# Index keys' tile moved to another buffer, and the loads around the GLU products reordered

## The chip, the cores and the metric

The kernel runs on one core of a Trainium2 chip. Time is device time in microseconds (us). Engines: TensorE (PE, matmuls and transposes), VectorE (DVE), ScalarE (ACT), GpSimd (POOL) and SyncE (SP, which issues nearly all DMAs here, in order). Matmul operands lie in SBUF, products come out in PSUM.

## The reference

One step of a one-layer hybrid encoder over 1024 prompt tokens and 32 sample tokens, width 1024. What matters here:

```python
h = rms_norm(x, g_norm) * (1 + scale) + shift
u, zs, q, k, v, za, qi, ki, wi, gm = split(h @ w_in)
ys = gelu(ssm(u))                              # 512 channels
ys = ys * sigmoid(ys @ w_glu + b_glu)          # GLU products
ys = ys * silu(zs)                             # silu factor
logits = relu(qi . [cache_kidx, ki]) / 8       # indexer, 8 heads of 64
score  = sum_heads(wi * logits)                # then the best 256 (136) keys per query
ya = attention(q, chosen k, v) * silu(za)
out = (sigmoid(g_s) * (ys @ w_ps) + sigmoid(g_a) * (ya @ w_pa)) @ w_o
```

## The kernel before

All products with float32 accuracy are made of three matmuls: each operand is a high part (rounded to the PE's fp32r format) plus a low part, and `mm3` adds high x high, high x low, low x high. Splitting costs a cast for the high part (`wh`, `ygH`, `yo[0]`, mostly on ScalarE) and a subtraction for the low part (`wl`, `ygL`, `yo[1]`, on VectorE or GpSimd).

A stream of jobs `Z` (class Stream) feeds PE. A Job is one product of 128 columns of a weight with all 1056 tokens, in 3 chunks of 352 columns; a chunk is 24 matmuls (8 row blocks x 3), for the GLU products 12 (4 x 3). Two PSUM buffers `pz` alternate, so a chunk can start when an evacuation one or two chunks earlier is done. While a job runs, the weight of the next one is split and that of the one after is loaded.

The stretch that the change touches comes after the SSM. There the jobs run in this order: `ki` (index keys and head weights, 72 columns, evacuated by ScalarE into the tile `zki`, L1073), `qi0` (index queries, evacuated by two copies on ScalarE and two subtractions on VectorE, L1066 to L1069), `glu0` to `glu3`, `qi1`. For the GLU, the four tiles y (128 channels each, gelu of the SSM's output) have been stored to DRAM (L991, `yD`) and are loaded again in token order (L1115, `yg`), then split into `ygH` and `ygL` (L70, L73). `gate_tile(q)` loads the two parts of silu(zs), stored by the silu jobs earlier (`zsD` is zs, `ztD` its tanh, made in tiles `zt` and `zth`), makes the silu factor z2 = (t2 + 1) * zs (L1089) and multiplies it by y (L1091). After each GLU chunk ScalarE takes the tanh (L1101), VectorE multiplies it in (L1102), and the product is split into `yo` (ScalarE and GpSimd) and stored (L1106). z2 has two buffers: tiles 2 and 3 are loaded at the end of glu0 and glu1 (`gate_tile(q + 2)`).

During qi1 PE transposes the cached index keys, loaded into `cki` (L1169, 128 partitions with pieces of 256 bytes, twice), and `zki` (L1174, L1183). `kid` collects all index keys, `kiH` and `kiL` are its parts, and the indexer's products follow (L1206, L1207). Pieces of w_mod are loaded between (`rpiece`, L1147) for a gate row (`grow`, L1155). Then a threshold search counts scores on ScalarE and VectorE (L1541, L1543); GpSimd clears its small tiles (L1518 to L1528).

PE's order is the order of the code (manual schedule). From L1038 to the search, the orders of SP, ACT, DVE and POOL are set by a scheduler from the code and a timeline that it works out, so a change of code moves instructions on all of them. Pools are stacks of SBUF: `kp` is opened when the SSM's pools have been closed, on the same bytes, so its first users wait for the last readers of what lay there. `stg` stays open for the whole kernel.

Of the kernel before, what the change touches and what calls it, by code (L numbers as in the profile page):

```python
# [7 lines left out]
F32 = mybir.dt.float32  # L8
# [9 lines left out]
NT = T + TS  # L18
# [40 lines left out]
def body(nc, tc, I, O, dbg=None):  # L59
    ctx = ExitStack()  # L60
    dbg = dbg or (lambda name, ap: None)
    I = {k: v for k, v in I.items()}
    te, ve, se, ge, sp = nc.tensor, nc.vector, nc.scalar, nc.gpsimd, nc.sync

    def f32(ap):
        return ap.bitcast(F32)

    def split(h, l, src, heng, leng):
        if heng is se:
            se.copy(h, src)  # L70
        else:
            heng.tensor_copy(h, src)
        leng.tensor_sub(l, src, f32(h))  # L73
# [3 lines left out]
    stg = ctx.enter_context(tc.tile_pool(name="stg", bufs=2))  # L77
# [613 lines left out]
    def silu_job(name, c0, dst, heng, leng, th_dst=None):  # L691

        def begin():
            zt = stg.tile([128, NT], F32, tag="stg", name="zt")
            zth = stg.tile([128, NT], F32, name="zth", bufs=1) if th_dst is not None else None

            def ev(n, ps):
                if th_dst is not None:
                    se.activation(zth[:, ns(n)], ps, AF.Tanh, scale=0.5)
                    se.copy(zt[:, ns(n)], ps)  # L700
                else:
                    th = stg.tile([128, G3], F32, tag="sth", name="th")
                    se.activation(th, ps, AF.Tanh, scale=0.5)
                    ve.scalar_tensor_tensor(zt[:, ns(n)], th, 1.0, ps, op0=ALU.add, op1=ALU.mult)
                if n == 2:
                    sp.dma_start(dst, zt)
                    if th_dst is not None:
                        sp.dma_start(th_dst, zth)
            return ev
        return Job(name, wcol(c0), begin, heng=heng, leng=leng)  # L710
# [343 lines left out]
    ysD = [[dram.tile([128, NT], F32, name=f"ys{h}D{q}") for q in range(4)] for h in "HL"]  # L1054
    stK = ExitStack()
    kp = stK.enter_context(tc.tile_pool(name="kp", bufs=1, side="right", reuse_waits="tile"))
    zki = kp.tile([72, NT], F32)
    QS = {}

    def qijob(j):  # L1060
# [18 lines left out]
    def tok(t):  # L1079
        return ((t[:, 0:1024].rearrange("p (c s) -> p c s", s=8), slice(0, 128)),  # L1080
                (t[:, 1024:NT].rearrange("p (c s) -> p c s", s=8), slice(129, 133)))

    yg, Z2 = [], []

    def gate_tile(q):
        z2, t2 = (gp.tile([128, NT], F32, name=n, bufs=b) for n, b in (("z2", 2), ("t2", 1)))
        sp.dma_start(z2, zsD[q])
        sp.dma_start(t2, ztD[q])
        ve.scalar_tensor_tensor(z2, t2, 1.0, z2, op0=ALU.add, op1=ALU.mult)  # L1089
        for v_, c in tok(z2):  # L1090
            ve.tensor_mul(v_, v_, yg[q][:, c])  # L1091
        Z2.append(z2)

    def glu_job(q):
        def begin():
            z2 = Z2[q]

            def ev(n, ps):
                c = ns(n)
                th = stg.tile([128, G3], F32, tag="sth", name="th")  # L1100
                se.activation(th, ps, AF.Tanh, scale=0.25, bias=bglu[:, q:q + 1])  # L1101
                ve.scalar_tensor_tensor(z2[:, c], th, 1.0, z2[:, c], op0=ALU.add, op1=ALU.mult)  # L1102
                yo = [gp.tile([128, G3], F32R, name=f"yo{h}", bufs=3) for h in range(2)]
                split(yo[0], yo[1], z2[:, c], se, ge)
                for h in range(2):
                    sp.dma_start(ysD[h][q][:, c], f32(yo[h]))  # L1106
                if n == 2 and q < 2:
                    gate_tile(q + 2)
            return ev
        return Job(f"glu{q}", w_glu[:, 128 * q:128 * q + 128], begin, kt=4, heng=se, leng=ve,  # L1110
                   rhs=lambda n, k: (ygH[k][:, ns(n)], ygL[k][:, ns(n)]))

    for q in range(4):
        yg.append(gp.tile([128, 8, NCH], F32, name=f"yg{q}").rearrange("p s c -> p c s"))
        sp.dma_start(yg[q].rearrange("p c s -> p s c"), yD[q])  # L1115
        for (h_, c), (l_, _) in zip(tok(ygH[q]), tok(ygL[q])):
            split(h_, l_, yg[q][:, c], se, (ge, ve)[(YS >> q) & 1])
    w_glu = I["w_glu"].rearrange("o d e -> (o d) e")
    for q in range(2):
        gate_tile(q)  # L1120
    Z.add(*(glu_job(q) for q in range(4)), qijob(1), *(gate_job(f, se, ve) for f in range(NS, NI - 1)))
    Z.add(qijob(2), qijob(3), gate_job(NI - 1, se, ve), hold=True)
    Z.until("glu3")
# [10 lines left out]
    ip = stI.enter_context(tc.tile_pool(name="ip", bufs=1, side="right", reuse_waits="tile"))  # L1134
# [28 lines left out]
    for hf_ in range(2):  # L1163
        sp.dma_start(kid[64 * hf_:64 * hf_ + 64, 0:1024], zki[0:64, 0:1024])
        sp.dma_start(kid[64 * hf_:64 * hf_ + 64, 1536:1568], zki[0:64, 1024:1056])
    cki = ip.tile([128, 4, 2, 64], F32)
    ckd = I["cache_kidx"].rearrange("a b (k p) d -> p (a b k) d", p=128)
    for hf_ in range(2):
        sp.dma_start(cki[:, :, hf_], ckd)  # L1169
    rpiece(0, None)  # L1170
    run(KF)
    pt = ps_t()
# [22 lines left out]
    for j in range(4):  # L1195
# [3 lines left out]
        for i in range(2, 9):  # L1199
            t0, m, k0, nk = (128 * i, 128, 0, 128 * (i + 1)) if i < 8 else (1024, 32, 1024, 544)  # L1200
            for e in range(2):
                h = 2 * j + e
                ps = ps_s()
                for a in range(0, nk, 512):
                    b = min(nk, a + 512)
# [468 lines left out]
    for k in range(len(seq) + 3):  # L1674
        it = at(k)
        if k in first:
            p, begin = first[k]
# [229 lines left out]
```

## Time and profile before

| what | value |
|---|---|
| time, median of 3 runs (lowest to highest) | 1058.91 us (1058.77 to 1058.99) |
| the profiled execution: its own time, its span | 1059.41 us, 1057.6 us |
| PE busy, share of the span | 996.2 us, 94% |
| DVE, ACT, POOL busy | 769.6, 541.9, 247.2 us |
| mean granted clock of PE, share of full speed | 0.98 |

How to read it: busy time of PE is from the start of a matmul to its modelled end, so back-to-back matmuls overlap and the step from one start to the next is the time that one takes. The granted clock is 1.00 at 2.4 GHz and 0.50 at 1.2 GHz. In a timeline, the bracket behind an instruction is how long its engine was idle before it and what ended that, as inferred.

### The profile page before, as it was taken

Reading aid. Unit: us, or ns where it says so; the run is one execution under the profiler, and the core shown is the slowest. Engines: PE = TensorE matmul, PEld = TensorE weight load, DVE = VectorE, ACT = ScalarE, POOL = GpSimd, SP = SyncE. Lnnn points to the kernel's source line nnn. Section 1 sums busy time; section 2 is a strip of 40 time slices with the busy share of each in tenths; the row PEclk is TensorE's granted clock in tenths of the full one; section 3 lists DMA queues with packets and bytes.
Section 4 is the critical chain, followed back from the end, with each engine's and each line's share of the span. In section 5 each row is a group of like instructions: output and inputs, shape, how many; then the busy total and the mean of one; then the engine's idle time right before and its main releaser. Section 6 shows DMA issues by size and latency. Waiting matters only on the chain.

```text
span 1057.6 us, 17197 instructions
## 1 busy us (share of the span) xinstructions
PE 996.2 (94%) x6194; PEld 927.6 (88%) x6194; DVE 769.6 (73%) x1756; ACT 541.9 (51%) x1164; POOL 247.2 (23%) x467
## 2 busy tenths in 40 slices
PE   4999999998979999898898999999999999999997
PEld 3899999997878889898898998899898988998786
DVE  4669798985755979988889945756657776786534
ACT  3642344545335656868895336655556555434111
POOL 3202400000240013243313442333222231340000
PEclk8999999998989999999998999999999999999999
DMA  9922722236673212223232242242133622854311
GB/s 304 273 69 85 228 77 79 78 102 196 196 231 111 61 61 73 79 71 111 81 101 83 81 144 56 77 131 61 51 101 106 222 80 76 277 162 139 123 67 60
DMA packets 125329, 126.00 MB, mean 119 GB/s; under 512 B 14400, under 2 KB 104980, under 8 KB 125244
## 3 DMA queue, kind: packets, MB, share of 16 engines
q1 hardware_dynamic: 124864, 124.59, 38.2%
q8 instruction: 49, 0.80, 0.3%
q14 instruction: 36, 0.29, 0.1%
q10 hardware_dynamic: 220, 0.28, 0.1%
q0 software_dynamic: 160, 0.03, 0.0%
HBM read 87.81 MB, written 36.50 MB: 118 GB/s over the span
## 4 chain that ended last, share of the span: by engine, by line
PE 65%; DVE 10%; ACT 9%; issue 7%; DMA 5%; SPq 2%; POOL 2%; POOLq 0%; ACTq 0%; DVEq 0%
PE pz L271 10%; PE pz L272 10%; PE pz L273 10%; ACT junkb L1541 5%; PE pss L1377 3%; PE psm L1876 3%; PE psm L1877 3%; PE psm L1878 3%; DMA wm<-in_w_mod 2%; DVE junk L1543 2%; PE pss L273 2%; PE pss L271 2%; PE pss L272 2%; PE pt L1470 2%; PE pspo L1489 2%
## 5 line engine op out<-in xcount | busy, mean ns | idle before, releaser
L271 PE MATMUL pz<-hH,wh 128*128 128x352 f32 (+1 forms) x776 | 261.8, 337 | 5.1 <-ACT zki L1073 4.4
L272 PE MATMUL pz<-hL,wh 128*128 128x352 f32 (+1 forms) x776 | 252.0, 325 | 0.0
L273 PE MATMUL pz<-hH,wl 128*128 128x352 f32 (+1 forms) x776 | 252.0, 325 | 0.0
L264 POOL TENSOR_TENSOR wl<-raw,wh 128x256 fp32r<-128x256 f32 (+1 forms) x184 | 133.2, 752 | 118.9 <-ACT wh L259 118.6
L271 PEld LDWEIGHTS pz<-hH,wh 128*128 128x128 f32 (+1 forms) x776 | 146.2, 188 | 9.3 <-ACT zki L1073 4.7
L272 PEld LDWEIGHTS pz<-hL,wh 128*128 128x128 f32 (+1 forms) x776 | 146.4, 189 | 1.7
L273 PEld LDWEIGHTS pz<-hH,wl 128*128 128x128 f32 (+1 forms) x776 | 145.9, 188 | 0.6
L1541 ACT ACTIVATE junkb<-sco,thr 128x896 bf16<-128x896 f32 (+3 forms) x128 | 103.6, 809 | 30.8 <-DVE thr L1606 21.5
L271 PE MATMUL pss<-hH,wh 128*128 128x352 f32 x304 | 103.3, 340 | 10.3 <-ACT tg L717 5.6
L273 PE MATMUL pss<-hH,wl 128*128 128x352 f32 x304 | 101.1, 333 | 0.4 <-POOL wl L264 0.4
L272 PE MATMUL pss<-hL,wh 128*128 128x352 f32 x304 | 101.1, 333 | 0.2 <-DVE hL L73 0.2
L1543 DVE TENSOR_SCALAR_CACHE_REDUCE junk<-sco,thr 128x1024 bf16<-128x1024 f32 (+2 forms) x96 | 96.9, 1010 | 2.3
L263 POOL CAST wh<-raw 128x256 fp32r<-128x256 f32 x88 | 35.1, 440 | 192.1 <-PE pz L272 110.9
L271 PEld LDWEIGHTS pss<-hH,wh 128*128 128x128 f32 x304 | 59.8, 197 | 14.0 <-POOL wh L263 6.1
L1473 DVE TENSOR_TENSOR PL<-pt,PH 128x512 fp32r<-128x512 f32 (+2 forms) x96 | 50.4, 552 | 27.9 <-ACT PH L1472 26.9
L1472 ACT CAST PH<-pt 128x512 fp32r<-128x512 f32 (+2 forms) x96 | 43.0, 482 | 43.0 <-PE pt L1470 39.8
L273 PEld LDWEIGHTS pss<-hH,wl 128*128 128x128 f32 x304 | 59.5, 196 | 0.8 <-POOL wl L264 0.8
L272 PEld LDWEIGHTS pss<-hL,wh 128*128 128x128 f32 x304 | 59.7, 196 | 0.4 <-DVE hL L73 0.4
L1209 ACT ACTIVATE rl<-pss 128x384 f32<-128x384 f32 (+6 forms) x56 | 41.1, 739 | 31.6 <-PE pss L1207 27.8
L1214 DVE SCALAR_TENSOR_TENSOR sco<-rl,wi,sco 128x384 f32<-128x384 f32 (+6 forms) x49 | 45.5, 937 | 15.9 <-ACT rl L1209 15.2
L1390 ACT ACTIVATE Sm<-Sm,mx 128x128 f32<-128x128 f32 (+8 forms) x68 | 52.7, 775 | 7.0 <-DVE mx L1383 7.0
L1878 PE MATMUL psm<-o,mL 128*128 128x512 f32 (+1 forms) x136 | 51.7, 381 | 0.0
(410 smaller groups left out, 2231.8 us busy)
## 6 DMA issues: line engine op xcount, KB each, us to landing
raw<-in_w_in SPq DMA_DIRECT2D x44, 512.0 KB
thD<-tg SPq DMA_DIRECT2D x16, 528.0 KB
tgl<-thD SPq DMA_DIRECT2D x16, 528.0 KB
wm<-in_w_mod SPq DMA_DIRECT2D x8, 1024.0 KB
rraw<-in_w_mod SPq DMA_DIRECT2D x4, 1024.0 KB
kd<-kd SPq DMA_DIRECT2D x32, 128.0 KB
xo<-in_x_prompt SPq DMA_DIRECT2D x8, 512.0 KB
rawo<-in_w_o SPq DMA_DIRECT2D x8, 512.0 KB
```

Of the source, the lines that this page charges most:

```text
L264: leng.tensor_sub(wl[:, c], raw[:, c], f32(wh[:, c]))
L271: te.matmul(ps, wh, xh, start=first, stop=False)
L272: te.matmul(ps, wh, xl, start=False, stop=False)
L273: te.matmul(ps, wl, xh, start=False, stop=last)
L1209: se.activation(rl[:m, :nk], ps[:m, :nk], AF.Relu)
L1214: ve.scalar_tensor_tensor(sco[i][:m, :nk], rl[:m, :nk], w, sco[i][:m, :nk], op0=ALU.mult, op1=ALU.add)
L1390: se.activation(P, P, AF.Exp, scale=-1.0, bias=self.mx, accum_out=self.rs)
L1472: se.copy(PH[:, b0:b1_, oc], src)
L1473: ve.tensor_sub(PL[:, b0:b1_, oc], src, f32(PH[:, b0:b1_, oc]))
L1541: se.activation(junkb[:m, :nk], x[:m], AF.Sign, bias=t, accum_out=cnt[:m, k:k + 1])
L1543: ve.tensor_scalar(junk[:m, :nk], x[:m], t, None, op0=ALU.is_lt, op1=ALU.add, accum_out=cnt[:m, k:k + 1])
L1878: te.matmul(ps, ml, wh, start=False, stop=last)
```

## The change

It moves the tile `zki` into the buffer that held `zth` in `stg` (its last reader there is the store of the fourth `ztD`), puts `cki` into pool `kp` in its place, and reorders the code: the first two `gate_tile` calls and the loads of `cki` stand ahead of the loads of y, and the product of z2 with y becomes a function of its own, `gate_y`, called after y has been split.

```diff
--- before.py
+++ after.py
@@ -692,7 +692,7 @@
 
         def begin():
             zt = stg.tile([128, NT], F32, tag="stg", name="zt")
-            zth = stg.tile([128, NT], F32, name="zth", bufs=1) if th_dst is not None else None
+            zth = stg.tile([128, NT], F32, name="zth", tag="zth", bufs=1) if th_dst is not None else None
 
             def ev(n, ps):
                 if th_dst is not None:
@@ -1054,7 +1054,8 @@
     ysD = [[dram.tile([128, NT], F32, name=f"ys{h}D{q}") for q in range(4)] for h in "HL"]
     stK = ExitStack()
     kp = stK.enter_context(tc.tile_pool(name="kp", bufs=1, side="right", reuse_waits="tile"))
-    zki = kp.tile([72, NT], F32)
+    zki = stg.tile([128, NT], F32, name="zki", tag="zth", bufs=1)[0:72]
+    cki = kp.tile([128, 4, 2, 64], F32)
     QS = {}
 
     def qijob(j):
@@ -1087,9 +1088,11 @@
         sp.dma_start(z2, zsD[q])
         sp.dma_start(t2, ztD[q])
         ve.scalar_tensor_tensor(z2, t2, 1.0, z2, op0=ALU.add, op1=ALU.mult)
-        for v_, c in tok(z2):
+        Z2.append(z2)
+
+    def gate_y(q):
+        for v_, c in tok(Z2[q]):
             ve.tensor_mul(v_, v_, yg[q][:, c])
-        Z2.append(z2)
 
     def glu_job(q):
         def begin():
@@ -1106,10 +1109,16 @@
                     sp.dma_start(ysD[h][q][:, c], f32(yo[h]))
                 if n == 2 and q < 2:
                     gate_tile(q + 2)
+                    gate_y(q + 2)
             return ev
         return Job(f"glu{q}", w_glu[:, 128 * q:128 * q + 128], begin, kt=4, heng=se, leng=ve,
                    rhs=lambda n, k: (ygH[k][:, ns(n)], ygL[k][:, ns(n)]))
 
+    for q in range(2):
+        gate_tile(q)
+    ckd = I["cache_kidx"].rearrange("a b (k p) d -> p (a b k) d", p=128)
+    for hf_ in range(2):
+        sp.dma_start(cki[:, :, hf_], ckd)
     for q in range(4):
         yg.append(gp.tile([128, 8, NCH], F32, name=f"yg{q}").rearrange("p s c -> p c s"))
         sp.dma_start(yg[q].rearrange("p c s -> p s c"), yD[q])
@@ -1117,7 +1126,7 @@
             split(h_, l_, yg[q][:, c], se, (ge, ve)[(YS >> q) & 1])
     w_glu = I["w_glu"].rearrange("o d e -> (o d) e")
     for q in range(2):
-        gate_tile(q)
+        gate_y(q)
     Z.add(*(glu_job(q) for q in range(4)), qijob(1), *(gate_job(f, se, ve) for f in range(NS, NI - 1)))
     Z.add(qijob(2), qijob(3), gate_job(NI - 1, se, ve), hold=True)
     Z.until("glu3")
@@ -1163,10 +1172,6 @@
     for hf_ in range(2):
         sp.dma_start(kid[64 * hf_:64 * hf_ + 64, 0:1024], zki[0:64, 0:1024])
         sp.dma_start(kid[64 * hf_:64 * hf_ + 64, 1536:1568], zki[0:64, 1024:1056])
-    cki = ip.tile([128, 4, 2, 64], F32)
-    ckd = I["cache_kidx"].rearrange("a b (k p) d -> p (a b k) d", p=128)
-    for hf_ in range(2):
-        sp.dma_start(cki[:, :, hf_], ckd)
     rpiece(0, None)
     run(KF)
     pt = ps_t()
```

What the scheduler makes of it, at three places. Line numbers of the new kernel are higher by 1 to 9. Names: `yD` and `yg` are y in DRAM and SBUF, `z` and `t` the two parts of the silu factor, `qis` the index queries, the number behind a name tells tiles apart. In brackets stand the semaphores that an instruction waits for, by the engine that raises them; the DMAs issued by SP take eight of them in turn, DMAHW0 to DMAHW7.

SP, from the store of the fourth y on, before:

```order
L991 DMA yD_1418<-Yq 128x8x133 [waits DMAHW7_49,DVE_49]
L1115 DMA yg_2723<-yD_1415 128x1064 [waits DMAHW0_49,PE_49]
L1115 DMA yg_2729<-yD_1416 128x1064 [waits DMAHW1_49,PE_49]
L1115 DMA yg_2735<-yD_1417 128x1064 [waits DMAHW2_49,PE_49]
L1115 DMA yg_2741<-yD_1418 128x1064 [waits DMAHW7_49,DMAHW3_49]
L1087 DMA z_2747<-zsD_217 128x1056 [waits DMAHW4_49]
L1088 DMA t_2748<-ztD_221 128x1056 [waits DMAHW5_49]
L1087 DMA z_2754<-zsD_218 128x1056 [waits DMAHW6_49]
```
And with the change:

```order
L991 DMA yD_1418<-Yq 128x8x133 [waits DMAHW7_49,DVE_49]
L1088 DMA z_2724<-zsD_217 128x1056 [waits DMAHW0_49,PE_49]
L1089 DMA t_2725<-ztD_221 128x1056 [waits DMAHW1_49,PE_49]
L1088 DMA z_2729<-zsD_218 128x1056 [waits DMAHW2_49]
L1121 DMA cki<-in_cache_kidx 128x4x64 [waits DMAHW7_49,DMAHW3_49]
L1121 DMA cki<-in_cache_kidx 128x4x64 [waits DMAHW4_49]
L1124 DMA yg_2736<-yD_1415 128x1064 [waits DMAHW5_49]
L1124 DMA yg_2742<-yD_1416 128x1064 [waits DMAHW6_49]
L1124 DMA yg_2748<-yD_1417 128x1064
L1124 DMA yg_2754<-yD_1418 128x1064 [waits DMAHW0_49]
```
The wait for the semaphore of the y store just above (DMAHW7) stood at the fourth load of y, behind three others; now it stands at the first load of `cki`, and all four loads of y come behind it.

VectorE, from the end of the SSM on, before:

```order
L73 TENSOR_TENSOR ygL_2719<-yg_2723,ygH_2715 128x1024 [waits DMAHW1_49,DMAHW0_49,Activation_49]
L73 TENSOR_TENSOR ygL_2719<-yg_2723,ygH_2715 128x32 [waits Activation_49]
L73 TENSOR_TENSOR ygL_2720<-yg_2729,ygH_2716 128x1024 [waits DMAHW1_49,Activation_49]
L73 TENSOR_TENSOR ygL_2720<-yg_2729,ygH_2716 128x32 [waits Activation_49]
L264 TENSOR_TENSOR wl<-raw,wh 128x512 [waits DMAHW7_49,PE_49,Activation_49]
L73 TENSOR_TENSOR ygL_2721<-yg_2735,ygH_2717 128x1024 [waits DMAHW2_49,Activation_49,Pool_49]
L73 TENSOR_TENSOR ygL_2721<-yg_2735,ygH_2717 128x32 [waits Activation_49]
L73 TENSOR_TENSOR ygL_2722<-yg_2741,ygH_2718 128x1024 [waits DMAHW3_49,Activation_49]
L73 TENSOR_TENSOR ygL_2722<-yg_2741,ygH_2718 128x32 [waits Activation_49]
L1068 TENSOR_TENSOR qis_2853<-pz,qis_2853 64x352 [waits DVE_49,DMAHW7_49,PE_49,Activation_49]
L1069 TENSOR_TENSOR qis_2854<-pz,qis_2854 64x352
L1089 SCALAR_TENSOR_TENSOR z_2747<-t_2748,z_2747 128x1056 [waits DMAHW5_49,DMAHW4_49]
```
And with the change (one weight split stands ahead of these rows):

```order
L1090 SCALAR_TENSOR_TENSOR z_2724<-t_2725,z_2724 128x1056 [waits DMAHW1_49,DMAHW0_49]
L1069 TENSOR_TENSOR qis_2856<-pz,qis_2856 64x352 [waits DVE_49,DMAHW7_49,PE_49,Activation_49]
L1070 TENSOR_TENSOR qis_2857<-pz,qis_2857 64x352
L1095 TENSOR_TENSOR z_2724<-z_2724,yg_2736 128x1024 [waits DMAHW5_49,DVE_49]
L1095 TENSOR_TENSOR z_2724<-z_2724,yg_2736 128x32
L73 TENSOR_TENSOR ygL_2720<-yg_2736,ygH_2716 128x1024 [waits Activation_49]
L73 TENSOR_TENSOR ygL_2720<-yg_2736,ygH_2716 128x32 [waits Activation_49]
L1069 TENSOR_TENSOR qis_2856<-pz,qis_2856 64x352 [waits PE_49,Activation_49]
L1070 TENSOR_TENSOR qis_2857<-pz,qis_2857 64x352
L73 TENSOR_TENSOR ygL_2721<-yg_2742,ygH_2717 128x1024 [waits DMAHW6_49,Activation_49]
L73 TENSOR_TENSOR ygL_2721<-yg_2742,ygH_2717 128x32 [waits Activation_49]
L73 TENSOR_TENSOR ygL_2722<-yg_2748,ygH_2718 128x1024 [waits DMAHW7_49,Activation_49,Pool_49]
```
The factor z of tile 0 and its product with y now stand ahead of the first low half of y, and the subtractions of qi0 between the low halves, where they stood behind all four.

ScalarE, from the second chunk of glu2 on (tile `yo_3128`, then `yo_3131`, is the first of the third GLU job), before:

```order
L70 CAST yo_3093<-z_2754 128x352 [waits DMAHW0_49,DVE_49,Pool_49]
L1101 ACTIVATE th<-pz,bglu 128x352 [waits PE_49,Activation_49]
L70 CAST yo_3128<-z_3020 128x352 [waits DMAHW3_49,DVE_49,Pool_49]
L259 CAST wh<-raw 128x1024 [waits DMAHW7_49,PE_49]
L70 CAST yo_3150<-z_3020 128x352 [waits DMAHW5_49,DVE_49,Pool_49]
L1101 ACTIVATE th<-pz,bglu 128x352 [waits PE_49,Activation_49] x2
```
And with the change:

```order
L1104 ACTIVATE th<-pz,bglu 128x352 [waits PE_49,Activation_49] x2
L259 CAST wh<-raw 128x1024 [waits DMAHW1_49,PE_49]
L70 CAST yo_3131<-z_3023 128x352 [waits DMAHW3_49,DVE_49,Pool_49]
L1104 ACTIVATE th<-pz,bglu 128x352 [waits PE_49,Activation_49]
L70 CAST yo_3153<-z_3023 128x352 [waits DMAHW7_49,DVE_49,Pool_49]
L1104 ACTIVATE th<-pz,bglu 128x352 [waits PE_49,Activation_49]
```
The weight split has moved ahead of the first cast, and the next tanh from behind the second cast to right behind the first.

On POOL the small memsets of the search have moved from behind two weight splits of the next stage to ahead of `kiL`; in the first round of the search, the five operations of `grow` on VectorE now stand between its counts. PE's order is unchanged.

## Rows read from the trace of the kernel before

**Rows 1.** the page, chain that ended last: share of the span by engine, then by line

```profile
PE 65%; DVE 10%; ACT 9%; issue 7%; DMA 5%; SPq 2%; POOL 2%; POOLq 0%; ACTq 0%; DVEq 0%
```

**Rows 2.** timeline, TensorE: start, duration (us), engine, line, operation, [idle before <-releaser]

```profile
249.15 0.57 PE L271 MATMUL pz<-hH,wh 128*72 128x352 f32 x1 [4.37 <-ACT zki L1073]
...
251.57 0.49 PE L273 MATMUL pz<-hH,wl 128*72 128x352 f32 x1
251.86 0.49 PE L271 MATMUL pz<-hH,wh 128*72 128x352 f32 x1
...
253.61 0.32 PE L271 MATMUL pz<-hH,wh 128*72 128x352 f32 x1
253.77 0.32 PE L272 MATMUL pz<-hL,wh 128*72 128x352 f32 x1
...
268.25 0.40 PE L271 MATMUL pz<-ygH,wh 128*128 128x352 f32 x1 [0.49 <-DVE qis L1069]
...
293.29 0.43 PE L271 MATMUL pz<-ygH,wh 128*128 128x352 f32 x1 [3.15 <-ACT th L1101]
...
311.17 0.68 PE L1174 MATMUL pt<-idf,cki 128*128 128x128 f32 x4 [3.08 <-DMA cki<-in_cache_kidx]
...
315.10 0.32 PE L272 MATMUL pz<-hL,wh 128*128 128x352 f32 x1
```

**Rows 3.** windows of 4 us: busy time per engine, then granted clock, DMA share, GB/s

```profile
248.00:252.00 4.00, 2.85 (x10) 2.35 (x11) 0.00 (x0) 2.73 (x3) 0.00 (x0) 0.50 0.97 378
268.00:272.00 4.00, 3.10 (x18) 2.85 (x19) 3.75 (x4) 1.70 (x4) 0.00 (x0) 1.00 0.30 87
312.00:316.00 4.00, 4.00 (x20) 3.93 (x19) 0.98 (x1) 0.92 (x3) 2.38 (x1) 0.62 0.54 209
```

**Rows 4.** timeline, ScalarE, GLU stage

```profile
248.65 0.80 ACT L1073 COPY zki<-pz 72x352 f32<-72x352 f32 x2 [7.66 <-DMA yg<-yD]
250.07 4.36 ACT L70 CAST ygH<-yg 128x1024 fp32r<-128x1024 f32 x4 [0.62 <-DMA yg<-yD]
...
290.97 0.48 ACT L70 CAST yo<-z 128x352 fp32r<-128x352 f32 x1 [3.99 <-DVE z L1102]
291.36 1.04 ACT L259 CAST wh<-raw 128x1024 fp32r<-128x1024 f32 x1
...
292.69 0.99 ACT L1101 ACTIVATE th<-pz,bglu 128x352 f32<-128x352 f32 x2
```

**Rows 5.** timeline, SP (the DMA issues), same stage

```profile
242.80 6.13 SPq L1115 DMA_DIRECT2D yg<-yD  x4
...
264.83 5.13 SPq L1088 DMA_DIRECT2D t<-ztD  x2
...
281.10 0.40 SPq L1087 DMA_DIRECT2D z<-zsD  x1
...
307.49 1.42 SPq L1169 DMA_DIRECT2D cki<-in_cache_kidx  x2
```

**Rows 6.** windows of 1 us: y loads (first), cki loads (second)

```profile
250.00:251.00 1.00, 1.00 (x6) 0.78 (x5) 0.00 (x0) 0.93 (x1) 0.00 (x0) 0.50 1.00 409
309.00:310.00 1.00, 0.00 (x0) 0.00 (x0) 0.00 (x0) 0.00 (x0) 0.00 (x0) 1.00 1.10 199
```

**Rows 7.** timeline, VectorE, GLU stage

```profile
258.16 4.28 DVE L73 TENSOR_TENSOR ygL<-yg,ygH 128x1024 fp32r<-128x1024 f32 x4 [1.05 <-issue]
262.45 0.52 DVE L1068 TENSOR_TENSOR qis<-pz,qis 64x352 fp32r<-64x352 f32 x1
...
264.83 2.20 DVE L1091 TENSOR_TENSOR z<-z,yg 128x1024 f32<-128x1024 f32 x2
...
268.36 1.26 DVE L1089 SCALAR_TENSOR_TENSOR z<-t,z 128x1056 f32<-128x1056 f32 x1 [0.25 <-DMA t<-ztD]
...
286.93 1.26 DVE L1089 SCALAR_TENSOR_TENSOR z<-t,z 128x1056 f32<-128x1056 f32 x1 [1.82 <-DMA z<-zsD]
```

**Rows 8.** timeline, ScalarE, first count of the threshold search

```profile
408.44 1.04 ACT L1541 ACTIVATE junkb<-sco,thr 128x896 bf16<-128x896 f32 x1 [4.26 <-POOL cnt L1519]
```

## Prediction

> **What bounds the kernel now.** I read the chain that ended last first: TensorE holds 65% of it [rows 1], so a microsecond counts where PE waits or runs slowly. Two such places lie in the stretch that the change touches; the reader should find them in PE's timeline [rows 2]. Before the last third of the index-key product (job ki) PE stands idle for 4.37 us until zki is copied, and before the transposes of the cached index keys it stands 3.08 us for the load of cki. A third wait, 3.15 us at 293.29, lies inside the GLU products. The windows give the second price [rows 3]: after the first wait the granted clock is 0.50 (the 1.2 GHz level), after the second 0.62, while between 268 and 272, with short waits only, it is 1.00 (2.4 GHz). At 1.2 GHz two matmuls start 0.29 us apart, at 2.4 GHz 0.16 (251.57 to 251.86 and 253.61 to 253.77, [rows 2]), so each slow one costs 0.13.
>
> Why zki is late shows on ScalarE [rows 4]: its first copy starts at 248.65 after 7.66 us idle. The profile names a load of y, but that copy needs no y. What had to end is the store of the fourth y, issued on SP just ahead of those loads: zki lies where that store's source buffer lay, and the four loads of y hold SP from 242.80 to 248.93 for the same reason, because the fourth reads what the store writes [rows 5].
>
> **The change, part by part.**
>
> *zki in the silu factor's buffer: removes the wait.* That buffer's last store went out with the silu jobs, a whole stage earlier, so the copies run as soon as PE has produced. PE goes on at 249.15 - 4.37 = 244.78; 24 matmuls of ki and 72 of the first index-query job (qi0) at 0.16 us are 15.4, so qi0 ends at 260.1. Before, it ended at 268.25 - 0.49 = 267.8 [rows 2]. PE comes to the GLU products 7.7 us early; whether that is worth anything depends on the y loads.
>
> *Loads of the silu parts and of cki ahead of y: adds a delay.* In SP's new order the two loads of cki stand ahead of all four loads of y, and the first of them takes over the wait for the y store, since cki now lies at the head of pool kp, where zki lay. So SP is free at about 248.6, spends 1.42 us on cki [rows 5], and issues the first y at about 250.1 instead of 242.8. When does it land? Before, the first y could be used at 250.07 [rows 4]; then the queue moves 409 GB/s [rows 6], 1.3 us for one load of 532 KB. The three silu loads now have the first places: 250.1, 251.4, 252.7. cki is 256 KB in small pieces, which moved at 199 GB/s [rows 6]: 1.3 us, to 254.0. The four y follow at 255.3, 256.6, 257.9 and 259.2. Bounds: earliest 253.6, if they pass the others (issue plus 3.5 us, as the load of t issued at 264.83 was usable at 268.36 [rows 5, 7]); latest 255.9 and a little more (5.8 us after issue, as for the z issued at 281.10 and used at 286.93). I take 255.3, the value nearest to the queue's own pace.
>
> *The DVE chain in its new order.* Once y lands VectorE has, without a gap: product with the silu factor 2.20, low half of y0 2.14 (half of 4.28), the two subtractions of qi0's second third, 0.52 each, and low halves of y1 to y3, 6.4 [rows 7]. That is 11.8 us, to 267.1. The first GLU chunk needs the last low half for its last matmuls and ends at about 267.7. Before, it ran from 268.25 for 12 x 0.16, to 270.2. Of the 7.7 us that PE was ahead, 2.5 are left.
>
> PE then waits in pieces from 260.1 to about 267. The rows show what follows such idle time: the clock was at 1.2 GHz after both long waits [rows 3]. I charge 8 slow matmuls, about 1.0 us, and 1.6 us are left. The Trainium skill, page "TensorE: Matmul & The Clock Gate", section "Part 1: The HAM clock gate (the "warmup" mystery)", says that the array falls to half its clock after idle time and gets it back only after sustained activity; the trace agrees (0.50 and 0.62 after the two waits). By that rule, bursts broken by waits could keep the clock down for longer than I charge; it speaks against the change.
>
> *The third silu factor and PE's wait at 293.29.* PE waits there for a tanh that ScalarE does at 292.69, behind a cast at 290.97 (waiting 3.99 us for DVE), a weight split at 291.36 and a second cast [rows 4]. The cast waits for a z2 whose load is issued at 281.10, after the first GLU job's products are done [rows 5]; these come 1.6 to 1.9 us earlier, and so does the load. In ScalarE's new order this tanh stands right behind the first cast: 292.69 - 291.36 = 1.3 us saved. Together 3.1 us. The wait stays about 3 us long, since PE also arrives earlier, so I credit nothing for the clock. Bounds for all of this part: a loss of 1 (y some 4 us later than taken) to a gain of 6.
>
> *cki long there: removes the second wait.* 3.08 us, plus the slow stretch: from 311.17 to 315.10 [rows 2], 3.9 us, PE did 10 full matmuls (1.6 at 2.4 GHz) and 8 small transposes (0.6 at most), so 1.7 more. Sum 4.8. Late next would be the load of w_mod behind cki on SP: it moves up by cki's 1.42, its user by 4.8, so at worst 3.4 come back. I take 0: it is 1,024 KB, 2.6 us at the queue's 409 GB/s.
>
> *Search.* The threshold search's small memsets on POOL now stand before the low half of the index keys. Before, the first count on ScalarE waited 4.26 us for them [rows 8]. But in VectorE's new order five operations of the gate row stand between the counts of that first round, so the round ends hardly sooner: 0, between 0 and 4.3.
>
> **Sum.** 3.1 + 4.8 = 7.9 us. The profiled execution took 1059.41, so 1051.5; it lies 0.5 above the median of the runs, 1058.91, so I predict 1051.0. PE is the bound from there to the search, so the gain is carried.
>
> **The rivals.**
> - *Early y, 0.20.* The y loads land at 253.6. That is 1.7 us more, and PE's third wait may then be too short to bring the clock down: 11 slow matmuls there, 1.4. Total 11.0: 1047.9. For it: an idle queue served a load in 3.5 us. Against: the queue is full then. The Trainium skill, page "DMA: Bandwidth & Descriptors", section "Queues, rings and completion order", says each DMA engine takes its descriptors in ring order; by that y stays behind cki. No run here shows two loads passing each other.
> - *Late y, 0.14.* y lands about 3 us later than taken, VectorE's chain starts so much later and the GLU part gains nothing. Only 4.8 remain: 1054.1.
> - *Starved TensorE, 0.03: slower.* The GLU products come in bursts behind DVE and the clock stays at 1.2 GHz. All 144 of their matmuls slow cost 144 x 0.13 = 18.7 us, so 1058.9 - 7.9 + 18.7 = 1069.7; it turns to a loss from 61 slow ones (7.9 / 0.13). For it: the idle stretch from 260 to 267. Against: 1.00 between 268 and 272 with waits in it [rows 3].
> - *The gain is not carried, 0.05.* From about 404 on the search could be paced by what does not move: no change, 1058.9. Against: what its first count waits for is POOL, whose splits wait for PE.
>
> **How the numbers follow.** The forecast has 0.58, with 1048.3 to 1053.6 as its own range (y between the bounds, w_mod late by up to 1). The range of 1047.2 to 1054.4 takes in the first two rivals' times and leaves out the rest and the tails. A measurement of this kernel tells about 0.2%, 2.1 us, from no change. Forecast, early and late y are faster: 0.92; not carried is the same: 0.05; starved is slower: 0.03.
>
> **What would show it.** Right: no PE wait at zki; the first two cki issues on SP near 248.6 and y behind them; the low halves of y ending near 267 on DVE; the first GLU chunk broken by waits, at a lowered clock; PE's third wait still 2 to 3 us; no wait at the transposes of cki, clock 1.00 there. Wrong: y usable before 254 or after 257, the clock low for more than a dozen GLU matmuls, or a new PE wait at w_mod or at the low half of the index keys.

## The result, and the profile after

| | before | with the change |
|---|---|---|
| median, first set (runs) | 1059.47 us (6) | 1050.24 us (6; 1047.26 to 1053.21) |
| ratio, 95% interval | | 0.9906 (0.9881 to 0.9931) |
| median, second set (e8; runs) | 1060.18 us (11) | 1049.91 us (6), ratio 0.9903 (0.9876 to 0.9930) |
| profiled execution: time, span, mean clock | 1059.41, 1057.6 us, 0.98 | 1053.21, 1051.4 us, 0.98 |

Predicted were 1051.0 us, range 1047.2 to 1054.4, faster: the time lies 0.8 below the prediction. The parts of the sum did not come out one by one; they missed in both directions, so that the total is this close is in part luck.

The profiled execution of the changed kernel is the slowest of its six, and it lost time ahead of the change. First SyncE (SP) in its timeline:

```profile
245.94 0.38 SPq L991 DMA_DIRECT2D yD<-Yq  x1
246.42 0.53 SPq L1088 DMA_DIRECT2D z<-zsD  x1
247.03 1.10 SPq L1089 DMA_DIRECT2D t<-ztD  x1
248.19 0.44 SPq L1088 DMA_DIRECT2D z<-zsD  x1
252.19 0.94 SPq L1121 DMA_DIRECT2D cki<-in_cache_kidx  x2
253.18 3.36 SPq L1124 DMA_DIRECT2D yg<-yD  x4
```

The store of the fourth y goes out at 245.94, in before at 242.31. PE's clock was low in another place of the first 50 us (0.51 in the window 36 to 44, where before has 1.00; in before it was 0.57 from 16 to 32). In e8, the same kernel again, it goes out at 242.28. So all comparisons below count from this store; 3.63 comes off the rows of after. Counted so, the changed kernel takes 9.8 us less to the end (e8: 10.2).

Counted so, the loads of cki are issued at 248.56 and the first y at 249.55 (predicted 248.6 and 250.1). ScalarE in the same stage:

```profile
244.61 0.45 ACT L1074 COPY zki<-pz 72x352 f32<-72x352 f32 x1
248.43 0.45 ACT L1074 COPY zki<-pz 72x352 f32<-72x352 f32 x1 [3.38 <-PE pz L273]
252.10 0.62 ACT L259 CAST wh<-raw 128x512 fp32r<-128x512 f32 x1 [3.22 <-DMA yD<-Yq]
...
259.15 2.28 ACT L70 CAST ygH<-yg 128x1024 fp32r<-128x1024 f32 x2 [2.14 <-DMA yg<-yD]
```

The copies of zki no longer wait for a load or store (3.38 is PE's own pace), where before ScalarE stood idle for 7.66 ahead of the first of them [rows 4]. For the 3.22 ahead of a weight split (`wh`) the profile names the store of y, but e8 does not bear that out:

```profile
248.45 0.62 ACT L259 CAST wh<-raw 128x512 fp32r<-128x512 f32 x1 [3.22 <-DMA yD<-Yq]
...
248.87 0.94 SPq L1121 DMA_DIRECT2D cki<-in_cache_kidx  x2
```

There the split starts 0.42 ahead of the loads of cki, which do wait for that store. In both executions it starts 0.03 behind the modelled end of the last ki matmul that reads the weight's high part, so the time fits a wait for PE to be done with that buffer. PE shows no wait there. In the profiled execution of the change the first y is usable at 259.15, that is 255.5. VectorE:

```profile
259.22 2.21 DVE L1095 TENSOR_TENSOR z<-z,yg 128x1024 f32<-128x1024 f32 x2 [1.12 <-DMA yg<-yD]
261.34 2.18 DVE L73 TENSOR_TENSOR ygL<-yg,ygH 128x1024 fp32r<-128x1024 f32 x2
263.53 0.52 DVE L1069 TENSOR_TENSOR qis<-pz,qis 64x352 fp32r<-64x352 f32 x1
...
264.62 6.21 DVE L73 TENSOR_TENSOR ygL<-yg,ygH 128x1024 fp32r<-128x1024 f32 x6
```

Its chain runs without a gap from 259.22 to 270.83 (255.6 to 267.2; predicted 255.3 to 267.1). TensorE and its windows (columns as in [rows 2, 3]):

```profile
264.74 0.40 PE L271 MATMUL pz<-ygH,wh 128*128 128x352 f32 x1 [0.99 <-ACT ygH L70]
...
266.69 0.43 PE L272 MATMUL pz<-ygL,wh 128*128 128x352 f32 x1 [1.07 <-DVE ygL L73]
...
268.74 0.66 PE L272 MATMUL pz<-ygL,wh 128*128 128x352 f32 x1 [1.31 <-DVE ygL L73]
...
270.77 0.66 PE L272 MATMUL pz<-ygL,wh 128*128 128x352 f32 x1 [0.78 <-DVE ygL L73]
...
293.71 0.43 PE L271 MATMUL pz<-ygH,wh 128*128 128x352 f32 x1 [1.09 <-ACT th L1104]
...
307.57 0.60 PE L1179 MATMUL pt<-idf,cki 128*128 128x128 f32 x4
...
314.88 0.64 PE L1161 MATMUL pg<-rraw,scP 128*32 128x512 f32 x4 [1.18 <-DMA rraw<-in_w_mod]
```

```profile
256.00:260.00 4.00, 4.00 (x27) 4.00 (x26) 1.82 (x3) 1.74 (x3) 0.00 (x0) 1.00 1.01 353
268.00:272.00 4.00, 2.21 (x5) 1.30 (x5) 4.00 (x6) 2.47 (x6) 0.00 (x0) 0.53 0.01 2
272.00:276.00 4.00, 3.63 (x12) 3.63 (x13) 3.92 (x5) 0.80 (x2) 1.16 (x1) 0.50 0.69 214
276.00:280.00 4.00, 4.00 (x19) 4.00 (x19) 1.68 (x4) 1.87 (x4) 1.93 (x2) 0.69 0.36 130
292.00:296.00 4.00, 2.91 (x18) 2.62 (x18) 4.00 (x7) 2.26 (x5) 2.72 (x2) 1.00 0.82 318
296.00:300.00 4.00, 4.00 (x27) 4.00 (x26) 3.97 (x3) 1.60 (x2) 2.12 (x2) 1.00 0.92 250
```

PE runs through the index-key products, then takes the first GLU chunk in four pieces, three of them behind a low half (1.07, 1.31, 0.78), with 0.53, 0.50 and 0.69 of the clock from 268 to 280: some 25 matmuls of the GLU products at 0.29 us. The third wait is 1.09 us instead of 3.15 [rows 2], and the clock stays at 1.00 behind it. In before it does not:

```profile
292.00:296.00 4.00, 2.71 (x13) 2.71 (x14) 3.57 (x3) 2.17 (x5) 2.57 (x3) 0.82 0.96 312
296.00:300.00 4.00, 4.00 (x21) 4.00 (x20) 3.85 (x6) 1.73 (x3) 0.80 (x1) 0.76 0.69 226
```

Ahead of that wait, with the change: the load of the third factor, VectorE's use of it, and ScalarE's cast and tanh:

```profile
283.87 0.53 SPq L1088 DMA_DIRECT2D z<-zsD  x1
...
288.65 1.26 DVE L1090 SCALAR_TENSOR_TENSOR z<-t,z 128x1056 f32<-128x1056 f32 x1 [1.51 <-DMA z<-zsD]
...
292.72 0.49 ACT L70 CAST yo<-z 128x352 fp32r<-128x352 f32 x1 [1.07 <-DVE z L1105]
293.11 0.55 ACT L1104 ACTIVATE th<-pz,bglu 128x352 f32<-128x352 f32 x1
```

At the transposes of cki (307.57) there is no wait; at 314.88 there is a new one for w_mod, 1.18 us. At the search, ScalarE's first count and VectorE's first counts:

```profile
395.67 1.04 ACT L1546 ACTIVATE junkb<-sco,thr 128x896 bf16<-128x896 f32 x1
...
400.04 1.28 DVE L1548 TENSOR_SCALAR_CACHE_REDUCE junk<-sco,thr 128x1024 bf16<-128x1024 f32 x1
...
401.36 0.68 DVE L1164 TENSOR_TENSOR grow<-pg,grow 2x512 f32<-2x512 f32 x1
401.97 0.76 DVE L1219 SCALAR_TENSOR_TENSOR sco<-rl,wi,sco 32x544 f32<-32x544 f32 x1
402.66 0.99 DVE L1548 TENSOR_SCALAR_CACHE_REDUCE junk<-sco,thr 128x768 bf16<-128x768 f32 x1
```

ScalarE's first count starts 3.9 us before its last score activation (`rl`, 399.53); before, it stood 5.3 behind that and waited for GpSimd [rows 8]. VectorE's counts stand among the last score and the additions of the gate row. In before its first count stood behind all of these, 6.2 behind the start of the last `rl`:

```profile
409.31 1.25 DVE L1543 TENSOR_SCALAR_CACHE_REDUCE junk<-sco,thr 128x1024 bf16<-128x1024 f32 x1
```

### The profile page after: what moved, and what is told of

Its sections match the earlier page's. It is cut to its first block, busy times and chain, and to the rows that moved or that the text cites. A ratio compares the mean times of both kernels' runs of the same rounds, so it can differ in the third digit from the quotient of the medians.

```text
span 1051.4 us, 17200 instructions
## 1 busy us (share of the span) xinstructions
PE 999.1 (95%) x6194; PEld 929.9 (88%) x6194; DVE 768.1 (73%) x1756; ACT 542.0 (52%) x1164; POOL 250.5 (24%) x467
## 4 chain that ended last, share of the span: by engine, by line
PE 66%; DVE 11%; ACT 10%; issue 5%; DMA 5%; SPq 1%; POOL 1%; ACTq 0%; POOLq 0%; DVEq 0%
PE pz L271 10%; PE pz L272 10%; PE pz L273 10%; ACT junkb L1546 5%; PE pss L1382 3%; PE psm L1881 3%; PE psm L1882 3%; PE psm L1883 3%; DMA wm<-in_w_mod 2%; PE pss L271 2%; PE pss L273 2%; DVE junk L1548 2%; PE pt L1475 2%; PE pss L272 2%; PE pspo L1494 2%
```

## The experiments

Every kernel has the same PE order. The scheduler moves rows on the other engines with each edit, so most edits change more than they name; e2 and e9 differ on GpSimd alone. The columns are microseconds gained against before, counted from the store of y, in the one profiled execution of each: at the start of the last GLU matmul, of the first transpose of cki, of the last score activation (`rl`), and at the end. "Search" is the time from the start of that `rl` to the start of the last of the 32 rounds' thresholds, 158.3 in before.

| run | ratio (95%) | GLU products end | transposes of cki | last score | end | search |
|---|---|---|---|---|---|---|
| the change | 0.9906 (0.9881 to 0.9931) | 4.7 | 7.2 | 7.2 | 9.8 | 155.6 |
| e8, again | 0.9903 (0.9876 to 0.9930) | 5.3 | 7.8 | 7.8 | 10.2 | 156.0 |
| e1 clears early | 0.9981 (0.9968 to 0.9995) | 1.6 | -0.2 | -0.6 | 1.7 | 155.3 |
| e2 cki only | 0.9932 (0.9913 to 0.9952) | 2.8 | 6.1 | 6.3 | 7.5 | 158.0 |
| e3 zki only | 0.9954 (0.9937 to 0.9971) | 3.4 | 1.6 | 0.8 | 4.6 | 154.8 |
| e4 y first | 0.9909 (0.9886 to 0.9932) | 3.2 | 6.5 | 7.5 | 10.1 | 155.5 |
| e5 cki elsewhere | 0.9911 (0.9885 to 0.9937) | 0.7 | 3.9 | 3.5 | 7.6 | 154.7 |
| e12, e5 again | 0.9906 (0.9885 to 0.9927) | 0.8 | 4.1 | 5.2 | 8.0 | 155.6 |
| e9 e2 and clears | 0.9909 (0.9889 to 0.9929) | 0.2 | 3.5 | 3.9 | 6.1 | 156.4 |
| e6 e4, 3 buffers | 0.9878 (0.9851 to 0.9906) | 6.4 | 8.5 | 8.6 | 12.5 | 155.3 |
| e11, e6 again | 0.9877 (0.9855 to 0.9899) | 6.0 | 8.8 | 8.4 | 12.7 | 154.0 |
| e7 change, 3 buffers | 0.9890 (0.9863 to 0.9918) | 4.8 | 7.2 | 7.5 | 12.1 | 154.2 |
| e10 e6, GpSimd | 0.9884 (0.9860 to 0.9907) | 6.8 | 9.6 | 8.4 | 12.2 | 154.9 |

Two steps hold steady from run to run. From the end of the GLU products to the transposes, the five executions of e2, e9, e5, e12 and e4, with cki early and two buffers for z2, gain 3.2 to 3.3 us each, near the 3.08 that PE waited there (the change and e8 gain 2.5). In the search, from that `rl` to the second round's threshold, all ten executions whose first counts stand early (all but e1, e2 and e9) take 2.6 us less than before, e1 and e9 0.7 less, and e2 nothing less; the 30 rounds behind them scatter (see the last section).

**e1: the clears alone.**

```diff
-    key = lambda n, dt: sel.tile([128, 7], dt, name=n)
+    key = lambda n, dt: scp.tile([128, 7], dt, name=n)
...
-                ge.memset(nse[:, c0 + k:c0 + k + 1], NSEL[i_])
...
```

(The tiles and all their memsets now stand ahead of the pool `ip`.)

> The kernel before, with the threshold search's small tiles (thr, cnt, nse, lim) put into an earlier pool and cleared on GpSimd ahead of the low half of the index keys; the orders of ScalarE, VectorE and SyncE stay as before. Theory (the search's earlier start in the changed kernel comes from where these clears stand): the first count on ScalarE no longer waits some 4 us for GpSimd, and the first round of the search ends about 2.5 us earlier; 2.5 us faster, about 0.9976 of before. Rival (the search's earlier start comes from other orders, of the gate row or of ScalarE's counts): the count starts early but the round ends when it did, 0 to 0.5 us.

Measured: 0.9981, 2.0 us faster. ScalarE's first count starts at 404.20 without a wait, but VectorE's order keeps its own behind the gate row:

```profile
404.20 1.03 ACT L1541 ACTIVATE junkb<-sco,thr 128x896 bf16<-128x896 f32 x1
...
404.87 2.84 DVE L1168 TENSOR_TENSOR grow<-pg,grow 2x512 f32<-2x512 f32 x4 [0.18 <-PE pg L1165]
...
408.89 1.26 DVE L1543 TENSOR_SCALAR_CACHE_REDUCE junk<-sco,thr 128x1024 bf16<-128x1024 f32 x1
```

The second round's threshold comes only 0.7 us sooner after the last score; the other 2.4 of the search come in later rounds. So the size is the theory's, the place is not, and whether the later rounds shorten through the clears is open: e6 and e11, the same kernel, differ by 1.2 there. ScalarE's and VectorE's orders are those of before, yet the GLU products end 1.6 us earlier, because the clock stays at 1.00 behind the third wait; the wait for cki takes it all back (4.66 instead of 3.08).

**e2: cki alone; e9: e2 with e1's clears.**

```diff
     zki = kp.tile([72, NT], F32)
+    cki = kp.tile([128, 4, 2, 64], F32)
...
     for q in range(2):
         gate_tile(q)
+    for hf_ in range(2):
+        sp.dma_start(cki[:, :, hf_], ckd)
...
```

> The kernel before, with only cki moved: its tile in pool kp behind zki, its loads on SyncE behind those of y and of the silu parts; zki stays where it was, and GpSimd's clears stand late as before. Theory (two separate gains): the 4.37 us wait for zki and the GLU products stay as before, the 3.08 us wait for cki goes with its slow stretch, 4.8 us less about 1.2 us for a new wait at w_mod: 3.6 us faster, ratio 0.9966. Rival 1 (the search gains with cki as well): 6 us faster, 0.994. Rival 2 (w_mod, now the last to come, takes most of it back): under 1.5 us.

Measured: 7.2 us faster, twice the theory's 3.6, though the search gained next to nothing (158.0). ScalarE's wait lists show what more has changed (the store of the fourth y raises DMAHW7; before, then e2):

```
L1073 COPY zki<-pz 72x352 [waits DMAHW0_49,DMAHW7_49,DVE_49,PE_49]
L1066 CAST qis_2853<-pz 64x352 [waits PE_49,Activation_49]
```

```
L1074 COPY zki<-pz 72x352 [waits DMAHW0_49,PE_49]
L1067 CAST qis_2856<-pz 64x352 [waits DMAHW7_49,DVE_49,PE_49]
```

The wait for the store has moved from zki's copy to the first cast of the index queries: with 2 KB more in `kp`, zki no longer lies on the bytes that the store reads. cki alone frees zki as well. PE's waits:

```profile
254.00 0.43 PE L271 MATMUL pz<-hH,wh 128*128 128x352 f32 x1 [2.00 <-ACT zki L1074]
...
261.49 0.40 PE L271 MATMUL pz<-hH,wh 128*128 128x352 f32 x1 [3.40 <-DVE qis L1070]
...
290.07 0.66 PE L271 MATMUL pz<-ygH,wh 128*128 128x352 f32 x1 [2.81 <-ACT th L1102]
```

zki's third copy is now only late because ScalarE casts y first (2.00); the next wait, 3.40, is qi0's subtraction behind VectorE's low halves. w_mod took nothing back. In this execution the GLU products end 2.8 us earlier; e9, with the same orders there, gains 0.2, so how much of the 2.8 comes from the freed zki is open.

> e2 with the search's small tiles in the earlier pool and cleared early, as in e1; the orders on SyncE, ScalarE and VectorE are those of e2, where the first counts stand behind the gate row's additions. Theory A (the clears' place is worth about 3 us to the search, whatever else is changed): the last threshold comes 2.5 to 3 us earlier than in e2, counted from the y store, so 9 to 10 us earlier than before, ratio 0.990. Theory B (in the changed kernel the 2.6 us come from counts that VectorE and ScalarE do between the last scores and the gate row's additions, and what e1 gained in later rounds was chance): the first count starts 4 us earlier, the first round ends at most 0.7 us earlier than in e2, the end within 1 us of e2's; ratio 0.993.

Measured: 0.9909, 2.4 us better than e2 by the ratios, whose intervals overlap. That speaks for A's size. The trace does not settle it: the search takes 156.4, 1.7 less than in e2; 0.7 of this lies in the first two rounds, as B has it, and 1.0 in later rounds, no more than e6 and e11 differ there. The last threshold, counted from the store, comes 0.7 later than in e2, not 2.5 to 3 earlier, since the GLU products ended 2.6 us later with the same orders: y was usable 0.7 later (249.42 against 248.72), the third factor 2.0 later (VectorE at 285.25 against 283.29), and the clock was at 0.50 from 292 to 296.

**e3: zki alone.**

```diff
-    zki = kp.tile([72, NT], F32)
+    zki = stg.tile([128, NT], F32, name="zki", tag="zth", bufs=1)[0:72]
...
```

> The kernel before, with only zki moved into the silu factor's buffer; the loads of y are first on SyncE as before, cki is loaded late as before. The clears on GpSimd stand early here too. Theory (the late y is what keeps the GLU part's gain at 3 us in the changed kernel): y is usable near 250, PE does the index keys' products without a wait and starts the GLU products about 5 to 6 us earlier than before, with its clock at 1.00; the cki wait stays at 3 us with its slow stretch; with the clears' 2.5 us it comes to 7 to 8.5 us faster, about 0.993. Rival 1 (the wait at zki only moves to another place in the GLU products, for the silu factor or a tanh): 2.5 us from the clears alone, 0.9976. Rival 2 (the clears are worth nothing): 5 to 6 us, 0.995.

Measured: 0.9954, 4.9 us, less than the theory's 7 to 8.5. The GLU products start 1.3 us earlier (theory 5 to 6) and end 3.4 earlier, but cki's loads are issued at 304.93, counted from the store only 2.1 earlier, and PE waits for them longer:

```profile
259.91 0.63 PE L271 MATMUL pz<-hH,wh 128*128 128x352 f32 x1 [3.37 <-DVE qis L1069]
...
290.93 0.43 PE L271 MATMUL pz<-ygH,wh 128*128 128x352 f32 x1 [2.97 <-ACT th L1101]
...
309.10 0.66 PE L1174 MATMUL pt<-idf,cki 128*128 128x128 f32 x2 [4.97 <-DMA cki<-in_cache_kidx]
```

The wait for cki grows from 3.08 to 4.97, so 1.6 are left at the transposes; the search's 3.5 make up the rest. The ratio is rival 2's number, but not by its reason: the search gains 3.5 (2.6 in its first two rounds). Rival 1 is half right: PE waits 3.37 for the subtraction of qi0 and 2.97 for the tanh instead.

**e5 and e12: cki early, zki behind the store.**

```diff
     zki = kp.tile([72, NT], F32)
+    cki = stg.tile([128, NT], F32, name="cki", tag="zth", bufs=1)[:, 0:512].rearrange("p (k a d) -> p k a d", k=4, a=2)
...
```

(The loads of cki move as in e2.)

> The kernel before, with cki loaded ahead of the GLU products as in e2, but its tile in the silu factor's buffer, so that zki keeps its old place at the head of pool kp. Theory (in e2 cki did two things: behind zki in kp it shifted zki off the y store's buffer, and it was there in time): zki waits for the y store again, 4.4 us, and the GLU products end when they did before, within 0.5 us (counted from the y store); the transposes come 3.4 us earlier, since cki is there; GpSimd's clears and the first counts stand early here, 2.4 us more; 5.5 to 6 us faster in all, about 0.9945. Rival (the 2.8 us that e2 gained by the end of the GLU products came from the new order on SyncE): the GLU products end 2.8 us earlier here too, and with the clears it is 8 us faster.

> e5 once more: cki early, zki still behind the y store. In e5's profile it took 7.6 us less than before from the index-key products on, while its timed ratio was 0.9911, as good as the whole change. Theory (freeing zki is worth 2 to 3 us on top, once cki is early): about 7.5 us faster, ratio 0.993. Rival (freeing zki is worth nothing on top, since what follows waits for the y loads and for the third silu factor): as the whole change, 0.9905.

Measured: PE waits 4.90 and 3.89 for zki again, and the GLU products end 0.7 and 0.8 earlier, against 2.8 in e2 (but 0.2 in e9, where zki is free too: within the scatter of single executions). The transposes come 3.9 and 4.1 earlier, the end 7.6 and 8.0, where e5's theory had 5.5 to 6. The ratios (0.9911, 0.9906) do not separate this from the whole change, and e12's interval just leaves out its theory's 0.993, so the times speak for e12's rival; the traces put freeing zki, and y's later place, on top of an early cki at 1.8 to 2.6 us at the end (9.8 and 10.2 against 7.6 and 8.0) and at 2.0 to 4.3 at the last score. Between nothing and that it stays open.

**e4: y first.**

```diff
-    for q in range(2):
-        gate_tile(q)
-    for hf_ in range(2):
-        sp.dma_start(cki[:, :, hf_], ckd)
     for q in range(4):
...
+    for q in range(2):
+        gate_tile(q)
+    for hf_ in range(2):
+        sp.dma_start(cki[:, :, hf_], ckd)
```

> The changed kernel with one order on SyncE undone: the four loads of y stand first, behind them the silu parts, behind these cki; zki and cki stay in their new places. Theory (gains add up, and y late behind cki costs about 3 us): 5 to 6 us at the GLU products, 3.6 at cki, 2.5 at the search, 11 to 12 us faster than before, ratio 0.989, and 2 to 3 us faster than the changed kernel. Rival (y's place does not matter, since the silu parts are then late and PE waits for a tanh instead): as the changed kernel, 0.9906.

Measured: 0.9909, as the change; the interval also holds the theory's 0.989, so the trace has to decide, and it speaks for the rival. The GLU products start 2.8 us earlier than before, but PE still waits 2.81 us for the tanh of the third job and goes on at 290.25, that is 290.0; the change goes on at 290.1. So with two buffers that wait, not y, sets when PE goes on. The GLU products end at 3.2 instead of 4.7 because the clock fell behind the longer wait.

**e6, e11: e4 with a third buffer for z2; e7: the change with one; e8: the change again.**

```diff
-(("z2", 2), ("t2", 1))
+(("z2", 3), ("t2", 1))
```

(Shown is the part of the line that changes.)

> e4 with a third buffer for the silu factor (z2), so that the factor of the third GLU job is loaded early and no longer waits for the first job's last products. Theory (PE's wait of 2.81 us in the third GLU job is the wait for that buffer, and it is what sets the end of the GLU products in all kernels so far): that wait is under 0.5 us, the clock stays at 1.00, the GLU products end 4 us earlier than in e4 (2.8 of wait, 1.4 of slow matmuls), of which w_mod's load takes some back; 1045 to 1046, ratio 0.987. Rival (VectorE has no room: its products with the factor then stand in the way of others): under 1 us better than e4.

> The changed kernel with the same third buffer for z2; cki stays ahead of y on SyncE. Theory (the some 3 us that the late y and the slow first GLU chunk cost were hidden by the wait for the silu factor behind them): with that wait gone they show, and the GLU products end 2.5 to 3 us later here than in e6, counted from the y store; 1048, ratio 0.9895, 2 us better than the changed kernel. Rival (y's place never mattered): as e6 within 0.5 us.

> The changed kernel once more, beside these three on the same chip. All theories: 1050 us, ratio 0.9906 as measured; PE's third wait near 1 us; from the y store to the transposes of cki about 61.7 us.

> e6 once more, beside e9 and e10 on the same chip. All theories: ratio 0.988, 12.5 us less from the y store to the end than before.

PE's waits in e6, then the slow stretch in e7, its last GLU wait and what ScalarE does ahead of that:

```profile
260.00 0.40 PE L271 MATMUL pz<-hH,wh 128*128 128x352 f32 x1 [3.34 <-DVE qis L1070]
...
282.41 0.43 PE L271 MATMUL pz<-ygH,wh 128*128 128x352 f32 x1 [1.59 <-ACT th L1104]
...
293.18 0.43 PE L271 MATMUL pz<-hH,wh 128*128 128x352 f32 x1 [0.95 <-ACT th L1104]
```

```profile
268.00:272.00 4.00, 3.63 (x12) 3.63 (x13) 3.97 (x4) 0.81 (x2) 1.16 (x1) 0.50 0.45 116
...
289.51 0.43 PE L271 MATMUL pz<-ygH,wh 128*128 128x352 f32 x1 [0.81 <-ACT th L1104]
...
287.96 1.05 ACT L259 CAST wh<-raw 128x1024 fp32r<-128x1024 f32 x1
```

In e6 the third wait is gone, two smaller ones for a tanh stand in its place (1.59, 0.95), and the GLU products end 3.2 us earlier than in e4 (theory 4). In e7 they end where they end in the change (4.8; 4.7 and e8 5.3), 1.2 to 1.6 behind e6 and e11 (theory 2.5 to 3), though the buffer is there. The slow start is not what keeps them there. Counted from the store and put on before's times, e7 starts the fifth GLU chunk at 277.2, e6 at 274.5; but at the eighth e7 starts at 283.0, e6 and e11 at 282.7 and 283.2, since these wait 1.6 for a tanh there and e7 does not. What e7 loses comes behind that, most of it in a wait of 0.81 at the eleventh chunk, for a tanh that stands on ScalarE behind a weight split. So the theory of e7 does not hold, nor does its rival to the letter, and 1.2 to 1.6 is less than e2 and e9 differ.

e6 and e11 are the fastest version here, 0.9878 and 0.9877; that is 2.3 to 2.9 us below the change by traces and ratios, with intervals that overlap. Of this 0.6 to 1.4 is there by the last score; the rest comes in the search and behind it, where executions scatter. e8 repeats the change within 0.6 us.

**e10: one low half on GpSimd.**

```diff
-MR, ML, YS, YW, HI, HG, JO, SF = (), 1, 15, 15, 0, 0, 8, (2, 2, 2, 1)
+MR, ML, YS, YW, HI, HG, JO, SF = (), 1, 11, 15, 0, 0, 8, (2, 2, 2, 1)
```

> e6 with the low half of the third y made on GpSimd instead of VectorE. Theory (VectorE's chain of low halves, not the arrival of y, sets when the index-query products and the GLU products go on): VectorE is free for the subtraction of qi0 2.1 us earlier, PE's wait of 3.34 us there falls to some 1.2 us, the GLU products start 2 us earlier and end 1.5 to 2 us earlier than in e6, counted from the y store; 1045 to 1046. Rival (GpSimd takes longer than 4 us for it, or slows VectorE beside it): GLU products start when they did, 0 to 0.5 us.

GpSimd, then PE's waits in e10:

```profile
256.39 2.88 POOL L73 TENSOR_TENSOR ygL<-yg,ygH 128x1024 fp32r<-128x1024 f32 x1 [25.58 <-ACT ygH L70]
...
264.06 0.40 PE L271 MATMUL pz<-ygH,wh 128*128 128x352 f32 x1 [1.47 <-DVE qis L1070]
...
309.53 0.64 PE L1161 MATMUL pg<-rraw,scP 128*32 128x512 f32 x4 [2.11 <-DMA rraw<-in_w_mod]
```

GpSimd takes 2.88 us for 1024 columns, VectorE 2.14 for all 1056 [rows 7]. The GLU products start 1.4 to 2.0 earlier than in e6 and e11, but end only 0.4 to 0.8 earlier, and PE then waits 2.11 us for w_mod, so the last score comes when it did. The chain theory holds for the start and is worth nothing at the end.

## Why the prediction was right, and where not

- **zki's wait goes; loads of y behind cki.** Right to 0.6 us at every point: cki 248.56, y issued 249.55, usable 255.5, VectorE's chain to 267.2, first GLU chunk to 267.9 (predicted 267.7). On the rivals early and late y: y came 6.0 us after its issue, in its place behind cki. The Trainium skill, page "DMA: Bandwidth & Descriptors", section "Queues, rings and completion order", has each engine take descriptors in ring order; the trace agrees (y usable at 255.5; by that order 255.3 was worked out).
- **"I charge 8 slow matmuls, about 1.0 us."** This step failed in size: some 25 (21 in e8), up to 3.3 us (0.13 each), more than the "dozen" that was to prove the forecast wrong. (2.5 less 1.0 is also 1.5, not the 1.6 that the text goes on with; that changes nothing.) The Trainium skill's rule that the text set against it (page "TensorE: Matmul & The Clock Gate", section "Part 1: The HAM clock gate (the "warmup" mystery)") was the better guide: the trace shows 0.53, 0.50, 0.69 behind the broken chunk. It did not cost that at the end, because the third wait took it up: e4, with y first and a clock at 1.00 in its first GLU chunks, goes on behind that wait at 290.0, the change at 290.1.
- **"The wait stays about 3 us long ... I credit nothing for the clock."** Failed, to the good: 1.09 us, and no slow matmuls behind it. PE goes on at 290.1 instead of 293.29, 3.2 earlier; the forecast was 3.1. The tanh order gave its 1.3; the third factor's 1.9 is right in part by luck: its load went out 0.9 earlier (e8 1.3; forecast 1.6 to 1.9), but landed sooner: VectorE starts at 285.0, before at 286.93. With 12 matmuls at 2.4 instead of 1.2 GHz (1.5) the GLU products end 4.7 earlier. This 1.5 belongs to the one execution of before: in e1, with the wait still 2.79, the clock stayed up as well.
- **cki, 4.8.** The size is right where nothing follows: from the end of the GLU products to the first product of the indexer, e12 and e4 take 18.4 us, 4.8 less than before (23.2). The change takes 20.4: 2.8 gained. The failed step is that the text takes 0 for w_mod: it took 1.18 (bound 3.4; a new wait there was a second sign that was to prove the forecast wrong), and PE waited 0.19 for VectorE in qi1; the rest of the 2.0 missing is spread over steps between matmuls without a wait that the profile lists.
- **Search, "0, between 0 and 4.3".** The 0 failed, not the bounds: 2.6 us between the last score and the end. VectorE's counts stand among the gate row's additions, not behind them, so the first two rounds end 2.6 sooner, in all ten executions with this order; early clears without it (e1, e9) give 0.7 there. Their searches are 3.1 and 2.0 shorter in all, but the rest lies in later rounds and may be scatter.
- **Carried to the end.** Right: 10.0 at the last threshold, 9.8 at the end.
- The sum was 7.9, made of 3.1, 4.8 and 0; the trace shows 4.7, 2.8 and 2.6, less 0.3 lost in the indexer: 9.8. So the parts missed by +1.6, -2.0, +2.6 and -0.3. Of the 9.8, 6.2 show in the profiled pair, because that execution lost 3.63 ahead of the change; the medians show 9.2 and 10.3. The gain was 1.3 to 2.4 larger than forecast; the median lies only 0.8 below the forecast because before's is 0.6 higher in this set (1059.47 against 1058.91).
- Not seen in the forecast: that cki in `kp` by itself frees zki (e2). What moving zki into the silu factor's buffer adds to that is open: by the ratios nothing (e9 0.9909, the change 0.9906), by the traces up to 4 us at the end (6.1 against 9.8 and 10.2), of which 1.9 is the order of the first counts (2.6 against 0.7).

## What to carry to other kernels

Before crediting a wait that goes, look for the next thing that sets the same end: here a freed product ran into a load that was issued late all the same (e3) or a two-buffer tile (e4), and a slow start was free ahead of such a wait. In a pool that is a stack, a new tile moves its neighbours, and with them their waits; read the wait lists, not the diff. When the start of each execution varies by microseconds, count from a marker just ahead of the change.

## What the runs showed of the hardware

- Behind an idle time of about the same length the clock fell in some executions and not in others: after the third wait it fell in before (3.15 us), e2 and e4 (2.81 each), e12 (3.09) and e9 (3.62), and stayed at 1.00 in e1 (2.79), e3 (2.97) and e5 (2.86). A forecast of a slow stretch behind such a wait is a chance of some 1.5 us, not a term.
- Kernels whose orders differ only on GpSimd (e2, e9) ended the GLU products 2.6 us apart, through loads that came 0.7 to 2.0 us later and the clock. A smaller difference between single profiles there says nothing.
- In the three executions whose first GLU chunk came in four pieces with waits of 0.8 to 1.3 us (the change, e8, e7), the clock fell to 0.50 and 21 to 25 GLU matmuls ran at 0.29 us.
- In the search, the 30 rounds after the second took 141.6 (e1) to 144.3 us (e8) in all with the same instructions, and 143.6 and 142.3 in e6 and e11, the same kernel; what sets the difference is open.
